# The low parts of r's and k's inputs and of the stage heads made on VectorE instead of GpSimd

## The chip, the cores and the metric

The kernel runs on one core of a Trainium2 chip. The metric is the device time of one execution in microseconds; the time before is the median of three runs. The core has TensorE (PE) for matmuls, whose weight loads are shown as PEld, VectorE (DVE), ScalarE (ACT) and GpSimd (POOL) for elementwise work, and SyncE (SP), which issues the loads. Each engine works through its own queue in order and waits on semaphores for the others.

## The reference, cut to what matters

A trunk of two layers on 256 tokens of 2048 channels, batch 1, all in float32. Layer 0 is RWKV-7 time mixing and a squared-ReLU MLP, layer 1 multi-head latent attention (MLA) and a second MLP. What the change touches is the inputs of the first projections and the inputs of three later stages:

```python
h = rms_norm(x, norm_g[l, 0]) * (1.0 + scale_m) + shift_m
xx = token_shift(h) - h
xs = h[None] + xx[None] * mu[:, None, None, :]        # r, k, v, w, a, g
rkv = jnp.einsum('jbtd,jde->jbte', xs[:3], w_rkv)
...
hs = rms_norm(x, kv_in_g); ckr = hs @ kv_down          # MLA's shared latent
...
h = rms_norm(x, norm_g[l, 2]) * (1.0 + scale_f) + shift_f
y = squared_relu_mlp(h, mlp_up[l], mlp_down[l])        # both layers
```

## The kernel before

TensorE multiplies in a rounded float32 format (fp32r). To keep the precision, each operand x is split in two: ScalarE casts the high part, hi = round(x) (L162), and another engine subtracts the low part, lo = x - hi (L163, the helper `hilo`). A product then is three matmuls, of hi with hi, hi with lo and lo with hi (L208 to L210, or L213 to L215 where the model's weights are the stationary operand). Weights are split in the same way as they arrive: a load of 128x2048 into raw or early, two casts whi and two subtractions wlo of 128x1024.

`hilo` takes the engine of the subtraction as an argument. It is VectorE but for two callers, which give GpSimd: the first stage for j = 0 and 1, the inputs of r and k (L499), and `affine4` (L1037).

The first stage (about 38 to 212 us) goes over 16 channel tiles of 128 in four groups of four (cb). Per tile it transposes the normed x (trx), makes h on ScalarE (L486) and d on VectorE (L488), and then six mixed inputs xs, in the order w, a, g, v, r, k: a scalar_tensor_tensor on VectorE (L491, three buffers), a cast on ScalarE, a subtraction. The parts for w, a, g are called xlh and xll and are multiplied at once (lr); those for v go to xsv, and the v projection (pv, V) of a group runs within the next group; those for r and k are kept for the second stage in tiles that the trace calls xs, like their inputs. In between stand the matmuls that make shift and scale from c (adap, modc), whose weights are loaded into raw and early.

Three later stages begin with a head: the first MLP (about 847 us), MLA (1589 us) and the second MLP (1902 us). In a head, for each half t of the tokens, 16 transposes (trt, L1021) scale and turn x. `affine4` takes four channel tiles at a time, applies scale and shift to four pieces of 128x128 in turn on ScalarE and VectorE into hc (128x512, two buffers), and splits hc into hh and hl (o1h and o1l in MLA). TensorE's order is written out by hand there: the transposes of t = 0, the products of its first two groups of four tiles, the same for t = 1, and then the products of groups three and four of both halves. Each group is 12 matmuls of 128x512. The weights for groups three and four are split in between (spare). In the head of MLA VectorE also makes xn from x (L1342).

Apart from such hand-written stretches the order in each engine's queue is set by a scheduler, which runs over the program with its own costs of the instructions.

Of the kernel before, what the change touches and what calls it, by code (L numbers as in the profile page):

```python
# [12 lines left out]
F32 = mybir.dt.float32  # L13
# [63 lines left out]
def trunk_kernel(ctx: ExitStack, tc: tile.TileContext, a, out, dbg=None):  # L77
    nc = tc.nc
    PE, DVE, ACT, POOL, SP = nc.tensor, nc.vector, nc.scalar, nc.gpsimd, nc.sync
# [24 lines left out]
    def rbank(name="rwt"):  # L104
        return banks["rw"].tile([P, 512], F32, tag="rw", name=name)
# [9 lines left out]
    def col(name, i):  # L115
        c0 = COLS[name] + i
        return pcol[:, c0 : c0 + 1]

    def cols(name, i, n):
        c0 = COLS[name] + i  # L120
        return pcol[:, c0 : c0 + n]
# [36 lines left out]
        DVE.scalar_tensor_tensor(y, u, 1.875 * g_, y, ALU.add, ALU.mult)  # L158
        return y

    def hilo(hi, lo, x, eng=DVE):
        ACT.copy(hi, x)  # L162
        return eng.tensor_sub(lo, x, hi.bitcast(F32))  # L163

    room_for = [None]

    def load(src, n=2048, ahead=False):
        raw = room_for[0]() if room_for[0] else None
        if raw is not None:
            SP.dma_start(raw[:, :n], src)  # L170
            return raw
        more = split.get("more")
        if more and not ahead:
            split["turn"] += 1
        raw = (more if more and not ahead and split["turn"] > EARLY else wp).tile([P, 2048], F32, tag="raw", name="raw")
        SP.dma_start(raw[:, :n], src)
        return raw
# [13 lines left out]
    def unit(src, n=2048, part=1024, room=None):  # L191

        raw = load(src, n)
        parts = []
        for c0 in range(0, n, part):
            m = min(part, n - c0)
            if room:
                hi, lo = room()
            else:
                hi = split["hi"].tile([P, 1024], F32R, tag="whi", name="whi")  # L200
                lo = split["lo"].tile([P, 1024], F32R, tag="wlo", name="wlo")
            hilo(hi[:, :m], lo[:, :m], raw[:, c0 : c0 + m])
            parts.append((hi, lo))
            pump(rate[0])
        return parts
# [6 lines left out]
    def mm3w(ps, wh, wl, xh, xl, start, stop):  # L212
        PE.matmul(ps, wh, xh, start=start, stop=False)  # L213
        PE.matmul(ps, wh, xl, start=False, stop=False)  # L214
        PE.matmul(ps, wl, xh, start=False, stop=stop)  # L215
# [63 lines left out]
    def ada_pe(l, m, cb, c32, pool):  # L279

        ps = banks["ad"].tile([P, 512], F32, tag="ad", name="adap")
        for g in range(4):
            raw = load(a["ada"][m, cb, g], ahead=True)
            for j in range(4):
                kt = g * 4 + j
                m_ = PE.matmul(ps[32 * j : 32 * j + 32, :], c32[:, kt, :], raw[:, j * 512 : (j + 1) * 512],
                               start=(g == 0), stop=(g == 3), tile_position=(0, 32 * j))
                last_ada[0] = m_.ins
            if g == 3:
                acc = pool.tile([P, 512], F32, tag="adap", name="adap", bufs=1)  # L290
                ACT.copy(acc, ps)
                mod_cols(l, m, cb, acc)
            yield
# [83 lines left out]
    with ExitStack() as s0:  # L377
# [8 lines left out]
        def xs_at(w, z, kt):  # L386
            return XS[kt // 4][:, 2 * w + z, kt % 4, :]

        with ExitStack() as s1:
# [34 lines left out]
            x = p2.tile([P, 2, D], F32, name="x")  # L424
# [25 lines left out]
            def value_part(cb, n):  # L450

                pss = [banks["pv"].tile([P, 512], F32, tag="pv", name=f"pv{t}") for t in range(2)]
                down_units([a["wv"][n, cb]], *xsv[cb], pss, list(range(4)))
                for t in range(2):
                    v = V[:, t, n * 512 : (n + 1) * 512]
                    if cb == 0:
                        ACT.copy(v, pss[t])
                    else:
                        DVE.tensor_add(v, pss[t], v)

            for cb in range(4):
                for z, n in (("lwa", 8 * DL), ("lg1", 1024)):
                    raw = load(a[z][cb], n)
                    lw_un[z] = [p3.tile([P, n], F32R, tag=z + "hl"[e], name=z, bufs=1) for e in range(2)]
                    hilo(*lw_un[z], raw[:, :n])
                at = iter(())
                if cb < 3:
                    at = chain(ada_pe(0, 1, cb + 1, c32, p3), ada_pe(0, 0, cb + 1, c32, p3))
                ks = slice(cb * 4, cb * 4 + 4)
                xsv[cb] = [p3.tile([P, 4, T], F32R, tag=f"xsv{z}", name="xsv", bufs=XV) for z in range(2)]  # L470
                XS.append(p1.tile([P, 4, 4, T], F32R, tag=f"xs{cb}", name="xs") if cb else xs0)
                spots.clear()
                spot_at[0] = 0
                DVE.scalar_tensor_tensor(A[:, ks], mods[0, 1][:, ks], 1.0, cols("norm_g", cb * 4, 4), ALU.add, ALU.mult)
                for kt in range(cb * 4, cb * 4 + 4):
                    if cb and kt % 4:
                        value_part(cb - 1, kt % 4)
                    next(at, 0)
                    next(at, 0)
                    ps = rbank("trx")  # L480
                    with tc.issue_after(first_done) if cb == 0 else nullcontext():
                        for t in range(2):
                            PE.transpose(ps[:, t * P : (t + 1) * P], x[:, t, kt * P : (kt + 1) * P], ident)
                    h = p6.tile([P, T + 1], F32, tag="h", name="h")
                    POOL.memset(h[:, 0:1], 0.0)
                    ACT.activation(h[:, 1:], ps[:, :T], AF.Identity, scale=A[:, kt : kt + 1], bias=mods[0, 0][:, kt : kt + 1])  # L486
                    d = p6.tile([P, T], F32, tag="d", name="d")
                    DVE.tensor_sub(d, h[:, :T], h[:, 1:])  # L488
                    for j in (3, 4, 5, 2, 0, 1):
                        xs = p6.tile([P, T], F32, tag="xs", name="xs")  # L490
                        DVE.scalar_tensor_tensor(xs, d, col("mu", j * KT + kt), h[:, 1:], ALU.mult, ALU.add)  # L491
                        if j >= 3:
                            hi = p6.tile([P, T], F32R, tag="xlh", name="xlh")
                            lo = p6.tile([P, T], F32R, tag="xll", name="xll")
                        elif j == 2:
                            hi, lo = (z[:, kt - cb * 4, :] for z in xsv[cb])
                        else:
                            hi, lo = xs_at(j, 0, kt), xs_at(j, 1, kt)
                        hilo(hi, lo, xs, DVE if j >= 2 else POOL)  # L499
                        if j == 3 or j == 4:  # L500
                            q = (kt % 4) * 2 * DL + (j - 3) * DL
                            wh, wl = lw_un["lwa"]
                            mm3w((pw if j == 3 else pa)[:DL], wh[:, q : q + DL], wl[:, q : q + DL], hi, lo, False, False)
                        elif j == 5:
                            q = (kt % 4) * 256
                            wh, wl = lw_un["lg1"]
                            for g in range(2):
                                mm3w(pg[g], wh[:, q + g * P : q + g * P + P], wl[:, q + g * P : q + g * P + P], hi, lo, False, False)
                value_part(cb, 0)
# [502 lines left out]
    x = xr  # L1012
# [11 lines left out]
    def affine4(t, g, ps, sc, bi, hi, lo, tp):  # L1024

        q, ks = slice(t * P, (t + 1) * P), slice(g * 4, g * 4 + 4)
        h = tp.tile([P, 4, P], F32, tag="hc", name="hc", bufs=2)
        for j in range(4):
            o, kt = slice(j * P, (j + 1) * P), g * 4 + j
            s, b = sc[:, kt : kt + 1], None if bi is None else bi[:, kt : kt + 1]  # L1030
            if j % 2 == t:
                DVE.tensor_scalar(h[:, j, :], ps[:, o], s, b, ALU.mult, ALU.bypass if bi is None else ALU.add)
            elif bi is None:
                ACT.activation(h[:, j, :], ps[:, o], AF.Copy, scale=s)
            else:
                ACT.activation(h[:, j, :], ps[:, o], AF.Identity, scale=s, bias=b)
        hilo(hi[:, ks, q], lo[:, ks, q], h, POOL)  # L1037

    def to_channels(xn, sc, bi, hi, lo, tp, tags=("rw",), kts=range(KT)):

# [522 lines left out]
```

## Time and profile before

| | |
|---|---|
| three runs | 2648.42 us median, 2644.48 to 2652.88 |
| profiled execution | 2649.35 us, span 2647.6 us |
| TensorE busy | 2541.5 us (96%) |
| VectorE busy | 1904.2 us (72%) |
| ScalarE busy | 1325.7 us (50%) |
| GpSimd busy | 134.2 us (5%) |
| chain that ended last | PE 87%, DVE 6%, ACT 3%, DMA 2%, issue 1%, POOL 1% |

Durations are those of one profiled execution. TensorE's share is an average over stages. What stands in brackets behind an instruction is how long its engine was idle ahead of it, and who ended that. L163 is the subtraction of `hilo` for all callers, so its instructions are told apart by the tiles they write.

### The profile page before, as it was taken

To read this page: it belongs to the slowest core of one execution; us is meant where nothing else is said; L and a number is where in the kernel's file an instruction comes from. 1 tells how busy PE (TensorE), PEld (TensorE's weight loads), DVE (VectorE), ACT (ScalarE), POOL (GpSimd) and SP (SyncE) were. 2 spreads that over 40 slices of the span, in tenths; PEclk is the share of its full clock that TensorE was granted. 3 is DMA by queue.
4 is the path that set the end of the run, shared out by engine and by line. 5 is a ranking of instruction groups with operands and counts; after the bars stand their busy time and mean duration, and the time that the engine had idled before them with its cause. 6 is when DMAs were issued, how large, how long until landed. Compare 5 with 4: busy or idle time off the path is not lost.

```text
span 2647.6 us, 43187 instructions
## 1 busy us (share of the span) xinstructions
PE 2541.5 (96%) x16968; PEld 2190.8 (83%) x16968; DVE 1904.2 (72%) x3647; ACT 1325.7 (50%) x2361; POOL 134.2 (5%) x206
## 2 busy tenths in 40 slices
PE   6989999999997999999999999999899999999998
PEld 3667788888776999989998977788798998899896
DVE  4687888888877688888888757777666555555555
ACT  3445666666745444444444546554544444444443
POOL 1120111011100100000000002000000000000000
PEclk7899999999998999999999999999999999999999
DMA  8755444444466588888888832646657555555553
GB/s 354 269 203 197 172 169 166 152 154 176 157 227 251 192 333 332 334 332 330 326 331 330 305 112 102 242 175 253 223 196 262 182 189 191 191 186 185 189 189 128
DMA packets 87901, 594.80 MB, mean 225 GB/s; under 512 B 10128, under 2 KB 14480, under 8 KB 16784
## 3 DMA queue, kind: packets, MB, share of 16 engines
q1 hardware_dynamic: 87696, 592.03, 60.7%
q8 instruction: 133, 2.18, 0.3%
q14 instruction: 72, 0.59, 0.1%
HBM read 589.89 MB, written 2.10 MB: 224 GB/s over the span
## 4 chain that ended last, share of the span: by engine, by line
PE 87%; DVE 6%; ACT 3%; DMA 2%; issue 1%; POOL 1%; SPq 0%; DVEq 0%; ACTq 0%; POOLq 0%
PE pup L215 9%; PE pup L214 9%; PE pup L213 9%; PE pd L208 9%; PE pd L209 9%; PE pd L210 9%; PE rk L213 2%; PE rk L215 2%; PE rk L214 2%; PE pm L657 2%; DVE wlo L163 1%; PE po L209 1%; PE po L210 1%; PE po L208 1%; PE pv L209 1%
## 5 line engine op out<-in xcount | busy, mean ns | idle before, releaser
L163 DVE TENSOR_TENSOR wlo<-raw,whi 128x1024 fp32r<-128x1024 f32 x729 | 868.5, 1194 | 476.6 <-ACT whi L162 474.5
L162 ACT CAST whi<-raw 128x1024 fp32r<-128x1024 f32 x729 | 743.2, 1022 | 887.6 <-PE pd L210 378.9
L215 PE MATMUL pup<-hh,wlo 128*128 128x256 f32 x1920 | 543.5, 283 | 0.0
L213 PE MATMUL pup<-hh,whi 128*128 128x256 f32 x1920 | 543.4, 283 | 0.0
L214 PE MATMUL pup<-hl,whi 128*128 128x256 f32 x1920 | 543.3, 283 | 0.0
L208 PE MATMUL pd<-whi,uh 128*128 128x512 f32 x1024 | 398.7, 389 | 0.0
L209 PE MATMUL pd<-wlo,uh 128*128 128x512 f32 x1024 | 398.5, 389 | 0.0
L210 PE MATMUL pd<-whi,ul 128*128 128x512 f32 x1024 | 398.4, 389 | 0.0
L309 DVE SCALAR_TENSOR_TENSOR raw<-raw,crow 128x1024 f32<-128x1024 f32 x320 | 387.3, 1220 | 9.0 <-DMA raw<-in_adat_dram 8.8
L213 PEld LDWEIGHTS pup<-hh,whi 128*128 128x128 f32 x1920 | 368.6, 192 | 0.5
L214 PEld LDWEIGHTS pup<-hl,whi 128*128 128x128 f32 x1920 | 368.5, 192 | 0.5
L215 PEld LDWEIGHTS pup<-hh,wlo 128*128 128x128 f32 x1920 | 368.6, 192 | 0.0
L210 PEld LDWEIGHTS pd<-whi,ul 128*128 128x128 f32 x1024 | 192.2, 188 | 40.1
L208 PEld LDWEIGHTS pd<-whi,uh 128*128 128x128 f32 x1024 | 192.3, 188 | 39.5
L209 PEld LDWEIGHTS pd<-wlo,uh 128*128 128x128 f32 x1024 | 192.3, 188 | 39.3
L213 PE MATMUL rk<-xs,whi 128*128 128x256 f32 x512 | 155.0, 303 | 2.8 <-ACT rS L584 2.2
L215 PE MATMUL rk<-xs,wlo 128*128 128x256 f32 x512 | 149.5, 292 | 2.0 <-DVE wlo L163 2.0
L214 PE MATMUL rk<-xs,whi 128*128 128x256 f32 x512 | 146.9, 287 | 0.0
L213 PEld LDWEIGHTS rk<-xs,whi 128*128 128x128 f32 x512 | 98.3, 192 | 13.9 <-issue 8.9
L215 PEld LDWEIGHTS rk<-xs,wlo 128*128 128x128 f32 x512 | 98.2, 192 | 4.7 <-DVE wlo L163 2.8
L214 PEld LDWEIGHTS rk<-xs,whi 128*128 128x128 f32 x512 | 98.4, 192 | 0.9
L721 DVE TENSOR_TENSOR xt<-ar,X 128x60 f32<-128x60 f32 (+14 forms) x240 | 49.3, 205 | 17.7 <-ACT ar L710 15.0
(432 smaller groups left out, 3825.5 us busy)
## 6 DMA issues: line engine op xcount, KB each, us to landing
raw<-in_adat_dram SPq DMA_DIRECT2D x160, 1024.0 KB, 6.8
raw<-in_up_dram SPq DMA_DIRECT2D x128, 1024.0 KB, 4.8
raw<-in_dn_dram SPq DMA_DIRECT2D x128, 1024.0 KB, 4.8
early<-in_ada_dram SPq DMA_DIRECT2D x17, 1024.0 KB, 11.7
raw<-in_wr_dram SPq DMA_DIRECT2D x16, 1024.0 KB, 4.8
raw<-in_wk_dram SPq DMA_DIRECT2D x16, 1024.0 KB, 4.8
raw<-in_wo_dram SPq DMA_DIRECT2D x16, 1024.0 KB, 4.8
raw<-in_mo_dram SPq DMA_DIRECT2D x16, 1024.0 KB, 5.6
```

The lines of the kernel that those rows point to most:

```text
L162: ACT.copy(hi, x)
L163: return eng.tensor_sub(lo, x, hi.bitcast(F32))
L208: PE.matmul(ps, lh, rh, start=start, stop=False)
L209: PE.matmul(ps, lh, rl, start=False, stop=False)
L210: PE.matmul(ps, ll, rh, start=False, stop=stop)
L213: PE.matmul(ps, wh, xh, start=start, stop=False)
L214: PE.matmul(ps, wh, xl, start=False, stop=False)
L215: PE.matmul(ps, wl, xh, start=False, stop=stop)
L309: DVE.scalar_tensor_tensor(raw[:, s], raw[:, s], 1.0, crow[:, s], ALU.mult, ALU.mult, accum_out=part[:, kt, half : half + 1])
L657: PE.matmul(pm[h][:, c * T : (c + 1) * T], lhs[hp, c * P : (c + 1) * P], AR[hp, c, :, :].rearrange("p x t -> p (x t)"), start=True, stop=True)
L721: DVE.tensor_tensor(xt[:, :, :n], ar[:, :, o : o + n], X[:, :, j : j + 1].broadcast_to([P, 4, n]), ALU.mult)
```

## The change

`hilo` loses its engine argument; every subtraction is VectorE's. No load, cast or matmul is added or removed.

```diff
--- before.py
+++ after.py
@@ -158,9 +158,9 @@
         DVE.scalar_tensor_tensor(y, u, 1.875 * g_, y, ALU.add, ALU.mult)
         return y
 
-    def hilo(hi, lo, x, eng=DVE):
+    def hilo(hi, lo, x):
         ACT.copy(hi, x)
-        return eng.tensor_sub(lo, x, hi.bitcast(F32))
+        return DVE.tensor_sub(lo, x, hi.bitcast(F32))
 
     room_for = [None]
 
@@ -496,7 +496,7 @@
                             hi, lo = (z[:, kt - cb * 4, :] for z in xsv[cb])
                         else:
                             hi, lo = xs_at(j, 0, kt), xs_at(j, 1, kt)
-                        hilo(hi, lo, xs, DVE if j >= 2 else POOL)
+                        hilo(hi, lo, xs)
                         if j == 3 or j == 4:
                             q = (kt % 4) * 2 * DL + (j - 3) * DL
                             wh, wl = lw_un["lwa"]
@@ -1034,7 +1034,7 @@
                 ACT.activation(h[:, j, :], ps[:, o], AF.Copy, scale=s)
             else:
                 ACT.activation(h[:, j, :], ps[:, o], AF.Identity, scale=s, bias=b)
-        hilo(hi[:, ks, q], lo[:, ks, q], h, POOL)
+        hilo(hi[:, ks, q], lo[:, ks, q], h)
 
     def to_channels(xn, sc, bi, hi, lo, tp, tags=("rw",), kts=range(KT)):
```

The scheduler puts the queues in another order with it; SP's order of loads stays the same. On VectorE's queue in the first group of the first stage (xs<-xs is the low part for r or k, xll that for w, a or g, d the difference of neighbouring tokens), the difference reads:

```order
 L163 TENSOR_TENSOR xsv<-xs,xsv 128x256
 L491 SCALAR_TENSOR_TENSOR xs<-d,pcol,h 128x256 x2
-L488 TENSOR_TENSOR d<-h 128x256 x2
+L488 TENSOR_TENSOR d<-h 128x256
+L163 TENSOR_TENSOR xs<-xs 128x256 x2
 L491 SCALAR_TENSOR_TENSOR xs<-d,pcol,h 128x256 x3
 L163 TENSOR_TENSOR xll<-xs,xlh 128x256 x3
 L491 SCALAR_TENSOR_TENSOR xs<-d,pcol,h 128x256 x3
 L163 TENSOR_TENSOR xsv<-xs,xsv 128x256
-L488 TENSOR_TENSOR d<-h 128x256
+L163 TENSOR_TENSOR xs<-xs 128x256 x2
+L488 TENSOR_TENSOR d<-h 128x256 x2
```

The pairs of new subtractions stand behind the xs of r and k that they read, the first one with one d between.

On the same queue in the first MLP's head, from the second dg on (dg scales the transposes of t = 1; the first two pairs of hl are those of t = 0):

```order
 L1105 TENSOR_SCALAR dg<-ident,rsy 128x128
 L163 TENSOR_TENSOR spare<-raw,spare 128x1024
+L163 TENSOR_TENSOR hl<-hc,hh 128x4x128 x2
 L1032 TENSOR_SCALAR hc<-trt,A_10028,mod_86 128x128 x2
 L163 TENSOR_TENSOR spare<-raw,spare 128x1024
 L1032 TENSOR_SCALAR hc<-trt,A_10028,mod_86 128x128 x2
-L163 TENSOR_TENSOR spare<-raw,spare 128x1024 x2
-L1032 TENSOR_SCALAR hc<-trt,A_10028,mod_86 128x128 x7
-L163 TENSOR_TENSOR wlo<-raw,whi 128x1024
+L163 TENSOR_TENSOR spare<-raw,spare 128x1024
+L163 TENSOR_TENSOR hl<-hc,hh 128x4x128 x2
```

The first pair of hl stands behind the first spare, the second between the third spare and the fourth.

## Rows read from the trace of the kernel before

**Rows 1.** The page's totals: busy us (share of the span), xinstructions.

```profile
PE 2541.5 (96%) x16968; PEld 2190.8 (83%) x16968; DVE 1904.2 (72%) x3647; ACT 1325.7 (50%) x2361; POOL 134.2 (5%) x206
```

**Rows 2.** GpSimd's groups: line, operation, out<-in xcount, busy us, mean ns, idle before.

```profile
L163 POOL TENSOR_TENSOR xs<-xs 128x256 fp32r<-128x256 f32 x32 | 30.6, 968 | 46.9 <-ACT xs L162 43.7 <-PE adap L286 3.1
...
L163 POOL TENSOR_TENSOR hl<-hc,hh 128x512 fp32r<-128x512 f32 x16 | 24.3, 1535 | 307.5 <-DVE hc L1032 288.1 <-ACT hh L162 19.4
L163 POOL TENSOR_TENSOR o1l<-hc,o1h 128x512 fp32r<-128x512 f32 x8 | 13.4, 1690 | 11.2 <-ACT o1h L162 9.8 <-DVE rsu L157 1.4
```

**Rows 3.** Stretches: PE, PEld, DVE, ACT, POOL busy; PEclk, DMA share, GB/s.

```profile
68.00:80.00 12.00, 10.45 (x36) 6.82 (x36) 9.28 (x17) 7.23 (x14) 0.10 (x1) 0.72 0.48 181
...
169.00:212.00 43.00, 37.94 (x187) 30.18 (x187) 42.45 (x84) 25.48 (x50) 11.90 (x16) 1.00 0.50 174
```

**Rows 4.** Order of time, first MLP's head, TensorE: start, us, instruction, idle before.

```profile
856.50 0.50 PE L210 MATMUL pup<-whi,hl 128*128 128x512 f32 x1 [1.05 <-POOL hl L163]
...
866.53 0.50 PE L208 MATMUL pup<-whi,hh 128*128 128x512 f32 x1 [1.14 <-ACT hh L162]
...
867.89 0.50 PE L210 MATMUL pup<-whi,hl 128*128 128x512 f32 x1 [0.62 <-POOL hl L163]
```

**Rows 5.** Order of time, TensorE, head of MLA.

```profile
1598.97 0.80 PE L210 MATMUL pl<-whi,o1l 128*128 128x512 f32 x1 [0.66 <-POOL o1l L163]
...
1600.41 0.63 PE L210 MATMUL pl<-whi,o1l 128*128 128x512 f32 x1
...
1611.36 0.50 PE L210 MATMUL pl<-whi,o1l 128*128 128x512 f32 x1 [0.62 <-POOL o1l L163]
1611.69 0.39 PE L208 MATMUL pl<-whi,o1h 128*128 128x512 f32 x1
```

**Rows 6.** Order of time, TensorE, second MLP's head.

```profile
1911.12 0.50 PE L210 MATMUL pup<-whi,hl 128*128 128x512 f32 x1 [1.55 <-POOL hl L163]
...
1921.63 0.50 PE L210 MATMUL pup<-whi,hl 128*128 128x512 f32 x1 [0.62 <-POOL hl L163]
```

**Rows 7.** VectorE's groups from 38 to 210 us.

```profile
L491 DVE SCALAR_TENSOR_TENSOR xs<-d,pcol,h 128x256 f32<-128x256 f32 x96 | 49.0, 552 | 3.6 <-POOL xs L163 3.2
L163 DVE TENSOR_TENSOR wlo<-raw,whi 128x1024 fp32r<-128x1024 f32 x19 | 23.6, 1277 | 5.3 <-ACT whi L162 5.3
L163 DVE TENSOR_TENSOR xll<-xs,xlh 128x256 fp32r<-128x256 f32 x48 | 18.7, 426 | 0.0
...
L163 DVE TENSOR_TENSOR wlo<-early,whi 128x1024 fp32r<-128x1024 f32 x8 | 9.5, 1223 | 2.9 <-ACT whi L162 2.9
...
L163 DVE TENSOR_TENSOR xsv<-xs,xsv 128x256 fp32r<-128x256 f32 x16 | 6.6, 414 | 2.2 <-ACT xsv L162 2.2
```

**Rows 8.** Order of time, VectorE, first stage.

```profile
41.32 1.27 DVE L491 SCALAR_TENSOR_TENSOR xs<-d,pcol,h 128x256 f32<-128x256 f32 x3
...
44.98 2.23 DVE L491 SCALAR_TENSOR_TENSOR xs<-d,pcol,h 128x256 f32<-128x256 f32 x3
47.13 1.08 DVE L163 TENSOR_TENSOR xll<-xs,xlh 128x256 fp32r<-128x256 f32 x3
```

**Rows 9.** Waits from 38 to 210 us: us in total, times, longest.

```profile
DVE xs L491 <- POOL xs L163: 3.2, 4, 1.3
```

**Rows 10.** Order of time, VectorE, before and in the first MLP's head.

```profile
834.19 1.28 DVE L960 TENSOR_TENSOR yo<-yo,G 128x512 f32<-128x512 f32 x2
...
854.10 1.22 DVE L163 TENSOR_TENSOR spare<-raw,spare 128x1024 fp32r<-128x1024 f32 x1
```

**Rows 11.** Order of time, VectorE, head of MLA.

```profile
1594.51 0.74 DVE L1342 TENSOR_SCALAR xn<-xr,rsy 128x1024 f32<-128x1024 f32 x1
...
1598.92 2.32 DVE L163 TENSOR_TENSOR spare<-raw,spare 128x1024 fp32r<-128x1024 f32 x1
...
1605.60 1.76 DVE L1342 TENSOR_SCALAR xn<-xr,rsy 128x1024 f32<-128x1024 f32 x1
```

**Rows 12.** Order of time, TensorE, first stage.

```profile
72.43 0.63 PE L210 MATMUL pv<-whi,xsv 128*128 128x512 f32 x1
```

## The prediction

> **What bounds the kernel now.** I read the engines' totals first, to see who can be the bound, then the groups of GpSimd, then the busy time by stretch, and last the order of time at the four places where GpSimd subtracts. TensorE is busy for 2541.5 of 2647.6 us, VectorE for 1904.2 [rows 1]: the kernel is TensorE's, and a change on the other engines counts only where TensorE stands for them. GpSimd's subtractions are three groups [rows 2]: 32 of 128x256 in the first stage (the low parts of r's and k's inputs) and 24 of 128x512 in the heads of three stages, 68.3 us together. The change touches no other instruction.
>
> The first stage (about 38 to 212 us) is one in which TensorE waits for VectorE: in its last quarter VectorE is busy for 42.45 of 43 us and TensorE for 37.94 [rows 3]. The heads are short stretches in which TensorE has nothing else to do. There the order of time shows it idle until a subtraction of GpSimd ends: 1.05 us before the matmul at 856.50, then 0.62, 0.66, 0.62, 1.55 and 0.62 at the five others like it, always the third matmul of a half [rows 4 to 6].
>
> **The change in the first stage.** Removed: 32 GpSimd subtractions. Added: 32 on VectorE. That engine already does the same form for xsv, at a mean of 414 ns, and three of it in a row (xll) take 1.08 us [rows 7, 8]. One more in a row costs (1.08 - 0.41) / 2 = 0.335 us, and 32 of them 10.7 us; each by itself at 0.414, 13.2 us.
>
> Given back: VectorE is slower while GpSimd subtracts. Three scalar_tensor_tensor instructions for xs take 1.27 us at 41.32, where GpSimd is idle, and 2.23 us at 44.98, where it is at work [rows 8]. How much this is over the stage, the groups tell [rows 7]. xs has a mean of 552 ns; three undisturbed take 1.27, and if each next one adds 0.40, the first is 0.47, so I take 475 ns as undisturbed: 96 x 0.077 = 7.4 us. wlo from raw has a mean of 1277 ns against 1223 for the same shape from early: 19 x 0.054 = 1.0. xll has 426 against xsv's 414: 48 x 0.012 = 0.6. Together 9.0 us. On top of that VectorE stood for GpSimd itself four times, 3.2 us, since xs has three buffers and GpSimd had not yet read the one wanted [rows 9]. This wait cannot come back: the reader is now on the same queue.
>
> So VectorE has 10.7 - 9.0 - 3.2 = -1.5 us in this stage. Nearly all of its work there lies ahead of a TensorE step or of a load, so I carry -1.5 to the end. The bounds: +10.0 us, if each subtraction costs 0.414 and nothing but the 3.2 us comes back, and -12.2, if all comes back and the subtractions fall into idle time of VectorE. I stay near the middle, since both terms are rows of this stage and the relief is measured on the very instructions that are slowed. A new wait: each subtraction waits for ScalarE's cast of its tile, and behind it in VectorE's queue stand the xs, xll and wlo instructions for which TensorE and the loads wait. The order puts the pair one d instruction behind the xs that it reads (first piece of the order). The xll triples stand just as close to their casts today, with idle time of 0.0 us ahead of them [rows 7]; hence I cost this wait at nothing. Without that cover it would be up to 0.4 us, a cast's length, for each of 16 pairs, 6.4 us, which lies inside the bounds.
>
> **The change in the heads.** Eight subtractions in each. VectorE takes 1.28 us for two 128x512 instructions with both inputs in SBUF [rows 10], by the same reading 0.68 for the first and 0.60 for the next; GpSimd's means are 1535 and 1690 ns [rows 2].
>
> First MLP. A spare of 1.22 us at 854.10 stands ahead of the first pair (second piece of the order), so the pair starts at 855.25 and the first low half is there at 855.93. The matmul at 856.50 comes 0.53 earlier [rows 4, 10]. The tiles hc have two buffers, and a subtraction frees one; at 0.60 instead of some 1.4 us apiece the next two are free 2 to 3 us earlier, so that the second half is bound by its transposes and no longer by GpSimd. They end today at 866.53 - 1.14 = 865.39, in the changed kernel 0.53 earlier, 864.86; two matmuls take 0.6 us, and the third stands at 865.45 instead of 867.89: -2.4 us. The other end, if ScalarE's high half moves by the 0.53 us alone: 866.00, a start 0.07 later and 0.68 for the low half give 866.75, -1.15.
>
> MLA. The matmul at 1598.97 comes 0.7 earlier, 0.68 instead of GpSimd's 1.3 behind the cast. In the second half five subtractions more, 3.0 us, stand in VectorE's queue in front of the low half that the matmul at 1611.36 needs; but a spare that takes 2.32 today instead of 1.22 and an xn that takes 1.76 instead of 0.74 lie in the same queue [rows 10, 11] and give back 2.1, and its two neighbours of the same kind more. I call that even, keep the 0.7 and add 0.6 for the second low half: -1.3. The other end is 0.
>
> Second MLP. 1911.12 becomes 1910.55, since a spare stands ahead of the pair again. In the second half the transposes end 0.55 earlier and the wait of 0.62 falls to nothing: -1.2 at 1921.63 [rows 6]. The other end is -0.6.
>
> Together -4.9 us, with -1.75 as the other end; 0, if the spare ahead of the pair waits for its load. Behind each head TensorE has 72 matmuls of products ready, so a gain there reaches the end, and the last subtractions, which the order puts behind a wlo, are wanted only behind 48 of them and cost nothing.
>
> **A rule that speaks against it.** In 169 to 212 us VectorE has 0.55 of 43 us left [rows 3]. The Trainium skill (Perfetto Trace Analysis, Optimizing Scalar/DVE Operations) says that where VectorE is saturated, work may be worth moving off it, even to GpSimd, and adds that the two share a read port, so that it might not help. By the first half of that sentence the time would be the second rival's; by the second half, the forecast's. The trace has 1.27 against 2.23 us for the second.
>
> **The sum.** -1.5 - 4.9 = -6.4 us on the profiled execution's own 2649.35 us (its span is 2647.6): 2643 us. That execution lies 0.9 above the median of 2648.42 and inside the three runs, 2644.48 to 2652.88. 0.3%, 7.9 us, is about what a measurement of this kernel can tell from no change: faster is below 2640.5, slower above 2656.4. The forecast is just inside no change.
>
> **Rivals.**
> 1. More than that, by TensorE's clock. Where TensorE stands in short pieces its clock falls: in 68 to 80 us the granted clock is 0.72 [rows 3], between the levels of 1.2 and 2.4 GHz, and a 128x512 matmul takes 0.63 us in such a stretch (1600.41) and 0.39 at full clock (1611.69) [rows 5]. 38 matmuls are slowed so: two stretches of 11 in the first stage, one of them around 72.43 us [rows 12], and 8 in each of the first two heads, all behind idle pieces that the change makes shorter. 38 x 0.24 = 9 us; with all of them gone 2634. For it: in the first MLP's head the idle pieces fall from 1.1 us to almost none. Against it: the third head has the same pieces and no slow matmul.
> 2. Slower: VectorE's queue pays for all. The place is the first stage, its last quarter above all. If xs and wlo are long for another reason than GpSimd, nothing comes back, and 13.2 - 3.2 = +10.0 us lie ahead of the low halves that TensorE multiplies, while the heads give nothing, because the pair stands behind a spare: 2659 us. It decides from where the relief in the first stage is under 10.7 - 3.2 - 4.9 = 2.6 of the 9.0 us. For it: the 42.45 of 43. Against it: the same three instructions are 0.96 us longer only where GpSimd works.
> 3. The change does what it says where nothing waits: the first stage is held by its ada matmuls and their loads, the heads by ScalarE's casts, which stay. Then the stage gives nothing and the heads 1.75: 2647.5.
>
> **How the numbers follow.** Forecast 0.50, its own range 2638 to 2648; rival 1 0.18; rival 2 0.15; rival 3 0.17. Faster by over 0.3%: two fifths of the forecast, 0.20, and rival 1, 0.38. Slower: rival 2 less its part under 2656.4, 0.13. No change: the remaining 0.49. The range goes from 2633, a little past rival 1, to 2656; past that lies most of rival 2, the 0.13 that is left out.
>
> **What the profile after would show.** GpSimd without a subtraction, busy for 68.3 us less; in the first stage xs at a mean near 475 ns and wlo from raw near 1223, and no wait of VectorE for GpSimd. If they stay at 552 and 1277, the relief was wrong, and rival 2 holds. In the heads the third matmul of each half comes right behind the second; if it waits for a VectorE subtraction that stands behind a spare, the heads' term was wrong. The stage of the r and k products should begin 1.5 us earlier, the first MLP's first full-width product 3.9, the second MLP's 6.4. If the first stage ends 5 us or more away from that on either side, the forecast fails there.

## The result and the profile after

The changed kernel takes 2636.49 us (median of 11 runs, 2627.95 to 2642.84), the kernel before, on the same chip, 2650.41 (11 runs, 2643.44 to 2668.03). The ratio is 0.9944, with an interval of 0.9924 to 0.9963: 10 to 20 us faster. The forecast was 2643, its range 2633 to 2656. Ratios leave out runs more than 1.5% above the fastest of their kernel; this matters only for the kernels cut short below.

The profiled execution is the longest of the 11, 2642.84 us, so stages are compared below, not spans. The totals:

```profile
PE 2544.0 (96%) x16968; PEld 2191.8 (83%) x16968; DVE 1911.7 (72%) x3703; ACT 1326.1 (50%) x2361; POOL 65.4 (2%) x150
```

Against [rows 1], GpSimd has lost 56 instructions and 68.8 us; VectorE has 56 more and is busy for only 7.5 us longer. VectorE's groups from 38 to 210 us tell why (line, operation, xcount, busy us, mean ns, idle before):

```profile
L491 DVE SCALAR_TENSOR_TENSOR xs<-d,pcol,h 128x256 f32<-128x256 f32 x96 | 41.4, 479 | 0.2
L163 DVE TENSOR_TENSOR wlo<-raw,whi 128x1024 fp32r<-128x1024 f32 x21 | 25.1, 1221 | 5.3 <-ACT whi L162 5.0
...
L163 DVE TENSOR_TENSOR xs<-xs 128x256 fp32r<-128x256 f32 x32 | 12.3, 418 | 0.1
```

xs has gone from 552 to 479 ns, wlo from raw from 1277 to 1221 [rows 7], and the wait for GpSimd [rows 9] is gone. The last row is the added work, 12.3 us. The first rk product, which marks the end of the first stage (first number of the stretch: its start), moved from 227.6 to 220.1 us:

```profile
L213 PE MATMUL rk<-xs,whi x512: 276/283/580, 220.1 to 699.2; 128*128 128x256 f32 x171
```

The heads, TensorE in the order of time, first the first MLP's, then MLA's, then the second MLP's:

```profile
858.51 0.50 PE L210 MATMUL pup<-whi,hl 128*128 128x512 f32 x1 [0.53 <-DVE hl L163]
...
867.56 0.50 PE L208 MATMUL pup<-whi,hh 128*128 128x512 f32 x1 [0.21 <-ACT hh L162]
...
868.29 0.50 PE L210 MATMUL pup<-whi,hl 128*128 128x512 f32 x1
...
1596.11 0.51 PE L208 MATMUL pl<-whi,o1h 128*128 128x512 f32 x1 [2.69 <-ACT o1h L162]
...
1905.33 0.50 PE L210 MATMUL pup<-whi,hl 128*128 128x512 f32 x1 [1.03 <-DVE hl L163]
```

Where TensorE waited for a low part of GpSimd's six times [rows 4 to 6], it waits for one of VectorE's twice, for 0.53 and 1.03 us. In the second half of the first MLP's head, the waits of 1.14 and 0.62 us have become 0.21 and none. The clock follows. The stretch around that place, before and then after (PE, PEld, DVE, ACT, POOL busy; then the granted clock):

```profile
866.00:872.00 6.00, 4.84 (x13) 3.58 (x14) 2.70 (x5) 4.15 (x8) 3.07 (x3) 0.72 0.04 15
```

```profile
867.00:873.00 6.00, 5.79 (x27) 4.36 (x26) 5.15 (x10) 5.63 (x10) 0.00 (x0) 1.00 0.33 141
```

A granted clock of 0.72 behind idle pieces has become 1.00, the level of 2.4 GHz, and the eight matmuls of 0.6 us there take 0.39. From its first transposition to the next step, the head lasts 38.27 us before and 34.55 after.

In MLA's head the first half has no slow matmuls left in this execution (other executions of the same head have them, see below), and the transposes of xn, which began at 1627.7, stand among the products from 1605.6 on. From MLA's first transposition to the second MLP's it is 312.94 us before and 309.16 after; the second MLP's head, to its own next step, 35.23 and 34.00. The heads gain 3.7, 3.8 and 1.2 us: 8.7 in all. The stages between them are equal within 0.4 us. The RWKV stage, from the first rk product to the first MLP's head, took 619.6 us before and 629.6 after, with no changed instruction in it. Whether the change did that was the first thing to test.

### The profile page after: what moved, and what is told of

Its sections match the earlier page's. It is cut to its first block, busy times and chain, and to the rows that moved or that the text cites. A ratio compares the mean times of both kernels' runs of the same rounds, so it can differ in the third digit from the quotient of the medians.

```text
span 2641.1 us, 43190 instructions
## 1 busy us (share of the span) xinstructions
PE 2544.0 (96%) x16968; PEld 2191.8 (83%) x16968; DVE 1911.7 (72%) x3703; ACT 1326.1 (50%) x2361; POOL 65.4 (2%) x150
## 4 chain that ended last, share of the span: by engine, by line
PE 87%; DVE 6%; ACT 3%; DMA 3%; issue 1%; POOL 0%; SPq 0%; DVEq 0%; ACTq 0%
PE pup L215 9%; PE pup L214 9%; PE pup L213 9%; PE pd L208 9%; PE pd L209 9%; PE pd L210 9%; PE rk L213 2%; PE rk L215 2%; PE rk L214 2%; PE pm L657 2%; DVE wlo L163 1%; PE pv L209 1%; PE pv L210 1%; PE pv L208 1%; PE ar L709 1%
## 5 line engine op out<-in xcount | busy, mean ns | idle before, releaser
L309 DVE SCALAR_TENSOR_TENSOR raw<-raw,crow 128x1024 f32<-128x1024 f32 x320 | 387.6, 1221 | 15.9 <-DMA raw<-in_adat_dram 15.8
```

Source lines behind the costliest of these rows:

```text
L309: DVE.scalar_tensor_tensor(raw[:, s], raw[:, s], 1.0, crow[:, s], ALU.mult, ALU.mult, accum_out=part[:, kt, half : half + 1])
```

## The experiments

All ratios are to the kernel before, timed beside it; a ratio of 0.001 is 2.6 us. Its median moved from 2649.3 to 2651.3 us between these series of runs, so kernels of different series are compared by their ratios.

| kernel | median us (runs) | ratio, interval |
|---|---|---|
| changed kernel | 2636.49 (11) | 0.9944, 0.9924 to 0.9963 |
| first stage's half alone | 2646.32 (12) | 0.9983, 0.9968 to 0.9999 |
| heads' half alone | 2640.11 (12) | 0.9965, 0.9950 to 0.9979 |
| changed, idle GpSimd work in the first stage | 2644.02 (12) | 0.9976, 0.9960 to 0.9991 |
| changed, first stage's subtractions twice | 2640.59 (12) | 0.9967, 0.9949 to 0.9985 |
| changed, extra work in the heads | 2645.68 (10) | 0.9978, 0.9964 to 0.9992 |
| changed, first groups in halves | 2628.73 (6) | 0.9920, 0.9899 to 0.9941 |

**The two halves.** Each is an edit of the kernel before. First the first stage's alone, which keeps GpSimd in the heads:

```diff
-                        hilo(hi, lo, xs, DVE if j >= 2 else POOL)
+                        hilo(hi, lo, xs)
```

> Only the first stage's half of the change: the 32 low parts of r's and k's inputs on VectorE, the 24 of the three heads left on GpSimd. TensorE's and VectorE's orders in the first stage are those of the changed kernel. Theory A (the first stage gains by what VectorE no longer shares with GpSimd, about 8 us, as in the profile of the changed kernel, and the heads gain about 10): the first rk product begins near 220 instead of 227.6, the heads last as before (38.3, 54.4 and 37.5 us), time 6 to 9 us under the kernel before, ratio 0.9966 to 0.9977. Theory B (the first stage's gain is given back in the stage behind it by a lower granted clock, as the 10 us lost there in the one profile suggest): the first rk product still near 220, but the RWKV stage again near 629 us, and the time within 2 us of before.

Then the heads' alone:

```diff
-        hilo(hi[:, ks, q], lo[:, ks, q], h, POOL)
+        hilo(hi[:, ks, q], lo[:, ks, q], h)
```

> Only the heads' half: the 24 low parts of the second MLP's, MLA's and the first MLP's heads on VectorE, the 32 of the first stage left on GpSimd. Theory A: the three heads shorten as in the changed kernel (3.7, 5.3 and 1.3 us), the first stage as before (rk begins near 227.6), time 8 to 11 us under before, ratio 0.996 to 0.997. The prediction's own terms: 4.9 us, ratio 0.9981. Rival 3 of the prediction: 1.75 us, ratio 0.9993. Theory B (a lower clock behind the first stage is what costs 10 us in the changed kernel): here the RWKV stage stays at 620 us since nothing ahead of it changed, and the time is as low as the changed kernel's or lower, ratio 0.994 to 0.996.

Measured: 4.5 us less (0.3 to 8.5) and 9.3 us less (5.6 to 13.3). Together 13.8, against the whole change's 14.8: within the intervals, the halves add up. The heads' interval leaves out both the prediction's 4.9 us and rival 3's 1.75. The first stage's decides nothing: it holds the prediction's 1.5 us, theory B's 2 and most of theory A's 6 to 9. With the first stage's half alone, the first MLP's head lasts 38.28 us, as before; with the heads' half, 34.56, as after. In the latter MLA's part is 310.65 us and the second MLP's head 33.99, so that the heads gain 3.7, 2.3 and 1.2: 7.2 us.

MLA's gain differs by 1.5 us between the two executions, 3.8 and 2.3, and the place is its first half: from its first transposition to the second half's it lasts 16.26 us before, 15.61 in the heads' half and 14.06 in the changed kernel. In the heads' half its matmuls behind the third are slow again:

```profile
1590.65 0.63 PE L209 MATMUL pl<-wlo,o1h 128*128 128x512 f32 x1
```

So they are in the two kernels that follow, whose first half lasts 15.48 and 15.63 us. In MLA 2.3 us are the change's; the 1.5 more came with the full clock, in one of the four executions with this head.

The profile of the heads' half has the old first stage, and yet:

```profile
L213 PE MATMUL rk<-xs,whi x512: 276/283/582, 218.5 to 692.7; 128*128 128x256 f32 x171
```

The old stage ended at 227.6 in one execution and at 218.5 in another, the new one at 220.1 and, with the first stage's half, at 215.6. So the 7.5 us between the first two profiles say nothing on the change: the stage scatters by more. The RWKV stage did too: 627.2 us with the first stage's half, 623.8 with the heads'.

**Idle GpSimd work, and VectorE work twice.** In the changed kernel, GpSimd gets 32 subtractions back that nobody waits for:

```diff
-                        hilo(hi, lo, xs)
+                        hilo(hi, lo, xs); j < 2 and POOL.tensor_sub(zf[:, :T], hi.bitcast(F32), hi.bitcast(F32))
```

> The changed kernel with 32 subtractions of 128x256 given back to GpSimd in the first stage, of tiles already made, into a tile that nobody reads, so that no engine waits for them and no buffer of xs hangs on them. TensorE's and VectorE's orders stay those of the changed kernel. Theory A (sharing slows VectorE): xs has a mean near 550 ns again instead of 479, the wlo of raw near 1270, and the first stage loses most of its 8 us: rk begins at 224 to 228, time 4 to 8 us over the changed kernel. Theory C (it is the new order on TensorE, the adap products earlier among the lr): the order is kept, so rk still begins near 220 and the time stays within 2 us of the changed kernel, though the xs are slow. Theory D (it was VectorE's waits for xs buffers that GpSimd held, 3.2 us): no such wait here, so 0 to 3 us lost.

Or VectorE makes each low part twice:

```diff
-                        hilo(hi, lo, xs)
+                        hilo(hi, lo, xs); j < 2 and DVE.tensor_sub(lo, xs, hi.bitcast(F32))
```

> The changed kernel with each of the 32 low parts of r's and k's inputs subtracted twice on VectorE, the second time over the first: 32 x 0.418 = 13.4 us of VectorE more in the first stage and nothing else. Prediction's term (the first stage ends by VectorE's queue, every subtraction paid at its pace): rk begins 10.7 to 13.4 us later, at 231 to 234, time 10 to 13 us over the changed kernel, which is at or above the kernel before. Rival (VectorE has slack for them between the loads and TensorE): rk within 4 us of 220, time within 4 us of the changed kernel. TensorE's order moves as well (about as many rows as the change itself moved), which could add a few us of either sign.

The first took 8.5 us more than the changed kernel (ratio 0.9976 to its 0.9944), as theory A wants, but its rk products began at 220.4, as theory C wants: one profile could not decide. The second took 6.1 us more, at a ratio of 0.9967, an amount that the two intervals leave anywhere from nothing to 13 us; its rk products began at 219.4, with no sign of 10.7 to 13.4 us, in one profile again.

**The first stage by itself.** To be rid of the rest's scatter, four kernels end behind the first stage and write V out; everything from the rk products on is left out.

```diff
-        if dbg:
-            dbg("V", V)
+        for t in range(2):
+            SP.dma_start(out[t * P : (t + 1) * P, :], V[:, t, :])
+        return
```

> The kernel before, ended behind the first stage: V's rows are written out and everything from the rk products on is left out. The orders on TensorE and VectorE up to there are those of the kernel before. It stands for the first stage alone, some 235 to 245 us, with the scatter of one stage in place of that of the whole kernel. To be read beside the same cut of the changed kernel.

> The changed kernel, ended behind the first stage in the same way. Theory A (the stage itself is shortened by the 7.5 us that the two profiles show): its median 5 to 9 us under the cut of the kernel before. Theory E (the stage's length scatters with TensorE's granted clock, 215.6 to 227.6 us at the rk products in six profiles, one of them 218.5 with the old first stage; the true difference is small): medians within 3 us of each other. The prediction's own term for the stage was 1.5 us less.

> The changed kernel with the 32 GpSimd subtractions that nobody waits for, ended behind the first stage as the two short cuts were (230.5 us with the old stage, 224.3 with the new). TensorE's and VectorE's orders are those of the changed kernel. Theory A (what the stage gained is VectorE's tiles no longer slowed beside GpSimd): 228 to 231 us, most of the 6.1 us gone, and the granted clock back near 0.91. Theory C (the gain is TensorE's new order, or the waits for xs buffers): 223 to 226 us, though xs has a mean near 530 ns again.

> The changed kernel with each of the 32 low parts of r's and k's inputs subtracted twice on VectorE, ended behind the first stage: 13.4 us more of VectorE. Prediction's term (every subtraction is paid at the queue's pace): 10.7 to 13.4 us over the changed cut, 235 to 238 us. Rival (VectorE has room for them): within 3 us of 224.3, as the whole kernel's profile suggests, where rk began at 219.4 with them and at 220.1 without. About 0.335 us of the end for each us of VectorE would give 4.5 us, 228 to 229.

| cut behind the first stage | median us (lowest to highest, runs) | ratio to the whole kernel before |
|---|---|---|
| before | 230.47 (226.29 to 235.90, 6) | 0.0859, 0.0854 to 0.0864 |
| changed | 224.34 (221.62 to 227.70, 6) | 0.0841, 0.0838 to 0.0844 |
| changed, idle GpSimd work | 231.28 (230.11 to 233.20, 4) | 0.0873, 0.0869 to 0.0877 |
| changed, subtractions twice | 227.61 (225.65 to 231.38, 6) | 0.0851, 0.0849 to 0.0854 |

By the medians the stage gains 6.1 us from the change, by the ratios 4.8: theory A's 5 to 9 or just below it, and more than theory E's 3 or the prediction's 1.5. The idle GpSimd work leaves the orders of TensorE, VectorE and ScalarE as they are in the changed kernel, and one instruction waits for it, on ScalarE, for 0.6 us. It alone takes away 6.9 us again by the medians, 8.5 by the ratios. That rules out theory C as the source of the gain, and theory D's 3 us at most: that VectorE's instructions are longer beside GpSimd's is enough for all of it. VectorE's groups in that kernel, then GpSimd's, 38 to 210 us:

```profile
L491 DVE SCALAR_TENSOR_TENSOR xs<-d,pcol,h 128x256 f32<-128x256 f32 x95 | 45.5, 526 | 0.1
L163 DVE TENSOR_TENSOR wlo<-raw,whi 128x1024 fp32r<-128x1024 f32 x20 | 24.3, 1240 | 6.6 <-ACT whi L162 6.6
...
L163 DVE TENSOR_TENSOR xs<-xs 128x256 fp32r<-128x256 f32 x32 | 13.9, 469 | 0.0
```

```profile
L499 POOL TENSOR_TENSOR zf<-xs 128x256 f32<-128x256 f32 x32 | 34.4, 1074 | 32.1 <-ACT xs L162 30.9
```

The same groups of the changed cut have 485, 1223 and 424 ns. VectorE is thus longer by 95 x 0.041 + 20 x 0.017 + 32 x 0.045 = 5.7 us, and the stage by 6.9. Subtracting twice makes VectorE longer by 32 x 0.421 = 13.5 us, and the stage by 3.3 (2.7 by the ratios): about a quarter of it, and a rough price, since TensorE's order is another one there. By the waits, what counts is not how long VectorE works but which instruction grows. The xs of w, a and g lead through ScalarE's cast and xll to the lr products; TensorE's waits for xll (us in total, times, longest) in the cut of before, then in that of the changed kernel:

```profile
PE lr L214 <- DVE xll L163: 3.1, 6, 0.7
```

```profile
PE lr L214 <- DVE xll L163: 0.4, 2, 0.2
```

With the idle GpSimd work the wait for xll is 1.0 us, and the one for xlh, the cast of the same xs, has grown from 2.2 us in the changed kernel's cut to 4.6:

```profile
PE lr L213 <- ACT xlh L162: 4.6, 6, 2.3
```

The low parts of r and k are wanted only by the rk products, behind the stage. This is read from waits; no run makes one of these instructions longer by itself. The mean granted clock moved with the stage: 0.885 to 0.933 in the six runs of the old cut (mean 0.907), 0.914 to 0.942 (mean 0.926) in the changed one. Within the old cut, the spans fall from 234.1 to 224.5 us as the clock rises, 0.2 us for each 0.001, so that 3.7 of the 6.1 us go together with the clock. Which of the two causes the other, these runs don't show.

**First stage and RWKV.** The same cut ahead of the first MLP; both MLPs and MLA are left out.

> The kernel before, ended ahead of the first MLP: x1 is written out, both MLPs and MLA are left out. First stage, RWKV and its projection, some 855 to 865 us. To be read beside the same cut of the changed kernel, and its mean granted clock too.

> The changed kernel, ended ahead of the first MLP in the same way. Theory A: 5 to 9 us under the cut of the kernel before, as much as behind the first stage. Theory B (what the first stage gains is given back in the RWKV stage by a lower clock, 629.6 us against 619.6 in the first two profiles): the two cuts equal within 2 us, whatever the shorter cuts differ by. Theory E (scatter): 0 to 4 us less, with no stage that gives anything back on the mean of the runs; the change's first half alone measured 3 us less in the median.

Inconclusive: 857.5 us (850.5 to 865.6, five runs) and 863.7 (850.4 to 865.6, five; a sixth, of 2383 us, is left out and stays unexplained), ratios 0.3226 (0.3216 to 0.3236) and 0.3223 (0.3208 to 0.3238). By the ratios that is 0.8 us less, give or take 4.8: a gain of 5 us and none both fit. Theory B is neither shown nor excluded here; the half alone, timed in the whole kernel, kept 4.5 us (0.3 to 8.5).

**Extra work in the heads.** In the changed kernel, each low part of the first MLP's and MLA's heads is followed by a GpSimd subtraction that nobody waits for; in the second MLP's, VectorE subtracts twice.

```diff
+    extra = [None]
...
         hilo(hi[:, ks, q], lo[:, ks, q], h)
+        if extra[0]:
+            extra[0](hi[:, ks, q], lo[:, ks, q], h)
...
+                if l == 0:
+                    extra[0] = lambda hi, lo, h: POOL.tensor_sub(ya[:, 0, :512].rearrange("p (a b) -> p a b", a=4), hi.bitcast(F32), hi.bitcast(F32))
+                else:
+                    extra[0] = lambda hi, lo, h: DVE.tensor_sub(lo, h, hi.bitcast(F32))
...
+            extra[0] = lambda hi, lo, h: POOL.tensor_sub(ckcq[:, 3, 0:2, :].rearrange("p a (b c) -> p (a b) c", b=2), hi.bitcast(F32), hi.bitcast(F32))
```

> The changed kernel with something added in each head. First MLP and MLA: eight subtractions of 128x512 on GpSimd, of the high parts just made, into a tile that nobody reads, so that they share with VectorE but make nobody wait. Second MLP: each of the eight low parts subtracted twice on VectorE. Theory A (the heads gained because VectorE and GpSimd no longer slow each other): the first MLP's head goes from 34.6 back to 37 to 38.3 us, MLA's from 49 to 50.7 back to 53 to 54.4. Theory F (it was the latency of GpSimd's own subtraction in the chain to the third matmul, 1.3 to 2.2 us against 0.68): both heads stay within 0.7 us of the changed kernel's. Second MLP: if VectorE's queue carries the head, 8 x 0.6 = 4.8 us more (36.2 to 41); if only the first low part of each half is waited for, 0.7 to 1.4 us more.

The first MLP's head is back at 38.88 us, longer than before; 1.6 of the 4.3 us are its eight slow matmuls, which are back behind a wait of 2.06 us. MLA's, to its next step, is at 52.2, against 49.13 in the changed kernel, both without slow matmuls (with them 50.7 in two other kernels with the same head, and 54.47 before). In the first head the orders of TensorE, VectorE and ScalarE are the changed kernel's. So theory F's forecast is wrong: GpSimd work that nobody waits for is enough to lose the whole gain of the first head, and most of MLA's. VectorE in the order of time, this kernel and then the changed one (start, us, instruction, two in a row):

```profile
849.53 2.98 DVE L163 TENSOR_TENSOR hl<-hc,hh 128x512 fp32r<-128x512 f32 x2
...
855.98 2.14 DVE L163 TENSOR_TENSOR hl<-hc,hh 128x512 fp32r<-128x512 f32 x2
```

```profile
857.77 1.29 DVE L163 TENSOR_TENSOR hl<-hc,hh 128x512 fp32r<-128x512 f32 x2
```

And GpSimd beside the first of these:

```profile
849.04 2.92 POOL L1102 TENSOR_TENSOR ya<-hh 128x512 f32<-128x512 f32 x2 [2.58 <-ACT hh L162]
```

It does not follow that this made the old first head long. There, of VectorE's large groups, only wlo, late in the head, was longer (1414 ns on the mean against 1220). The spare, 1422 ns on the mean with the extra work, had in the kernel before:

```profile
L163 DVE TENSOR_TENSOR spare<-raw,spare 128x1024 fp32r<-128x1024 f32 x4 | 4.8, 1218 | 0.0
```

What the old head shows in its place are waits for the buffers of hc that GpSimd's subtractions held, 2.0 us on VectorE and 3.4 on ScalarE, as the prediction had it. In the old head of MLA, spare and xn had 1483 and 1183 ns, in the new one 1218 and 746: there both count.

In the second MLP's head, two waits grew by 1.2 us each, and the head by 2.4 (34.00 to 36.43), more than the 0.7 to 1.4 expected: of the eight extra subtractions, 5.2 us, only those ahead of a first low half are paid.

```profile
1905.41 0.50 PE L210 MATMUL pup<-whi,hl 128*128 128x512 f32 x1 [2.24 <-DVE hl L1104]
...
1916.45 0.50 PE L210 MATMUL pup<-whi,hl 128*128 128x512 f32 x1 [1.20 <-DVE hl L1104]
```

**A faster version.** The waits left stand ahead of the first products of a half. So the first group of each half is split in two pieces:

```diff
-        hilo(hi[:, ks, q], lo[:, ks, q], h)
+        for k in ((0, 2), (2, 4)) if g == 0 else ((0, 4),):
+            kk = slice(g * 4 + k[0], g * 4 + k[1])
+            hilo(hi[:, kk, q], lo[:, kk, q], h[:, k[0] : k[1], :])
```

> The changed kernel with the high and low parts of the first group of each half of each head made in two pieces of 128x256 (6 copies and 6 subtractions more), so that the first product can start when two of the four columns are split. The waits left in the changed kernel's heads are 1.6 and 0.5 us in the first MLP, 2.7 in MLA, 0.3 and 1.0 in the second MLP. Theory F (the chain of copy, subtraction and product sets the start): each first wait falls by 0.3 to 0.7 us, the three heads by 1 to 2.5 us together, time 0 to 3 us under the changed kernel. Rival (VectorE's and ScalarE's queues carry the heads, and a small instruction costs nearly as much as a large one): heads equal or up to 1.5 us longer. In the first MLP TensorE's order moves too, a few of the next products stand earlier.

2628.73 us, at a ratio of 0.9920 (0.9899 to 0.9941): the fastest here. Against the changed kernel's 0.9944 that is 6.4 us, but the two intervals overlap, so that the times alone don't show that it is faster. The profile speaks for it. Its heads, measured as above, are 33.91 us, then 307.28 and 31.32; from the first MLP's head to MLA's it is 702.81 against 703.70, since products of the next unit fill the first head. That is 0.6 + 1.9 + 2.7 + 0.9 = 6.1 us less, past what theory F allowed. TensorE waits for no low or high part in either MLP's head; the second MLP's first products:

```profile
1892.14 0.48 PE L208 MATMUL pup<-whi,hh 128*128 128x512 f32 x1
...
1892.69 0.40 PE L210 MATMUL pup<-whi,hl 128*128 128x512 f32 x1
```

## Why the prediction was right, and where it was wrong

The time lies in the range, 6.5 us under the forecast, and 1.5 us under the forecast's own range (2638 to 2648): it is rival 1, with its 2634, that made the range wide enough. The likeliest side, no change within 0.3%, did not come: it is 0.56% faster. The mechanism was the forecast's, in both places, and both terms were too small.

- Relief of VectorE: right. xs at 479 ns (forecast 475), wlo from raw at 1221 (1223), no wait for GpSimd. The new wait for ScalarE's casts, costed at nothing, is 0.1 us in all.
- First stage, -1.5 us: mis-sized. The cuts measured -6.1 by the medians and -4.8 by the ratios, 4.6 and 3.3 from the forecast; the first two profiles, -7.5, lie 6.0 from it, past the 5 us at which it was to fail, but the stage scatters by more than that. The step that failed is the one that summed VectorE's queue and carried the sum to the end at full price. The 10.7 us of added work cost about a quarter of that (3.3 for 13.5), while the relief is worth at least its own length (6.9 for 5.7). An estimate from these, 2.6 us paid and 6.9 given back, is -4.3, or -7.5 if the 3.2 us of waits come back in full too: the cuts lie in between. Rival 2, which charged all of the added work, fell for the same reason: a VectorE that is busy for 42.45 of 43 us [rows 3] was not the path for every instruction in its queue. Rival 3 fell with the 4.8 to 6.1 us.
- First MLP, -2.4: mis-sized, -3.7. The first half's third matmul came 0.51 earlier after its transposition (forecast 0.53), the second half's 2.1. The other 1.6 are the eight slow matmuls, which the forecast left to rival 1.
- MLA, -1.3: mis-sized, -2.3, and -3.8 in the execution without the eight slow matmuls. The first half gave 0.65 (forecast 0.7), the second 1.6 (forecast 0.6). The 3.0 us of subtractions called even with the relief were more than even: in the second half both of TensorE's waits, 0.54 and 0.62 us, are gone, and the transposes of xn lie among the products.
- Second MLP, -1.2: right, -1.2.
- The sign that was to show the heads' term wrong, a third matmul that waits for VectorE behind a spare, came in two heads, for 0.53 and 1.03 us. It contradicted the sum, which had the spare ahead of the pair: the third matmuls came 0.51 and 0.53 us earlier, as summed (0.53 and 0.57).
- Rival 1: partly right. Its eight matmuls in the first head came back in four executions of four, those in MLA's in one, and in the first stage the granted clock rose. Over 94 runs, of the first five kernels of the table and of the kernel before, 0.001 of mean granted clock goes with 2.15 us; the changed kernel's runs have 0.9831 on the mean against 0.9807, so that some 5 of its 13 to 15 us go with the clock.
- The rule of the Trainium skill (Perfetto Trace Analysis, Optimizing Scalar/DVE Operations): its second half, that VectorE and GpSimd share a read port, so that offloading between them might not help, agrees with the traces, with 1.29 against 2.14 and 2.98 us for the same two subtractions; that a port is the reason, no run here shows. Its first half, that work may be moved off a saturated VectorE, failed here.

Open is how much of the first stage's 5 to 6 us outlasts the RWKV stage, whose length scatters from 619.6 to 634 us.

## What to carry to other kernels

Work on GpSimd can cost time though nobody waits for it: here VectorE's instructions beside it grew (xs from 485 to 526 ns), and the price stands in their means. Not every one pays: V from pv kept 688 ns in the same two kernels. What it costs the end depends on which chain the slowed instructions head. A busy engine is a path only for the instructions that somebody waits for: double the work in question and look before charging it in full. Read a stage's gain from several executions: the old first stage, which the change shortens by some 5 us, ended at 227.6 us in one profile and at 218.5 in another. Where a consumer waits for the first of several pieces, make the first piece small: in one profile that took some 6 us off the heads and what follows them.

## What was not expected of the hardware

Two VectorE subtractions of 128x512 took 1.29 us alone and up to 2.98 beside two of GpSimd, which took 2.92: more than half of GpSimd's time was added to VectorE's. And the same stage of the same kernel, cut behind it, took 226.3 to 235.9 us from run to run, with a mean granted clock of 0.933 in the shortest and 0.885 in the longest, more scatter than this change is worth there.
